# Turning queries and keys of a cross-decoder by VectorE squares and ScalarE copies instead of TensorE transposes

## The chip, the cores and the metric

The kernel runs as one program on one core of a Trainium2 chip. The metric is the device time of that program in microseconds (us). A core has a matrix engine (TensorE, PE in the profile; its weight loads are PEld), a vector engine (VectorE, DVE), a scalar engine (ScalarE, ACT), a general engine (GpSimd, POOL) and a sequencer that here only issues transfers (SyncE, SP). Each engine works through its own list of instructions in order, and semaphores join them.

## The reference, cut to what matters

A decoder trunk of two layers works on 256 tokens of width 2048, in fp32. Layer 0 is gated linear attention with a gated ConvFFN. Layer 1, where the change lies, makes shared keys and values from the output of layer 0 and attends to them, again with a ConvFFN behind. With 256 tokens there is one block of keys, so its attention is plain causal attention of 16 heads of width 128 with a bias by distance:

```python
kv = rms_norm(x, norm_w) @ w_kv;  k, v = split(kv)
k = rms_norm(k.reshape(B, S, 16, 128), k_norm_w)          # norm over each head's 128
q = rms_norm((rms_norm(x, norm_w) @ w_q).reshape(B, S, 16, 128), q_norm_w) * 128 ** -0.5
s = einsum(q, k) + bias_table[:, rel_bucket(t - j)]       # causal: -inf where j > t
o = einsum(softmax(s), v).reshape(B, S, 2048) @ w_out
```

The scores need queries and keys with the head's 128 elements on the partitions, while the projections leave them with tokens on the partitions. So each head's queries and keys are turned (transposed), 256 tokens by 128 each.

## The kernel before

**The stream of weights.** All weights come in halves of 128x1024 by transfers that SP issues into `wraw` (ten buffers). Each half is split for TensorE: ACT makes the high part `whi` (a cast, L143), DVE the rest `wlo` (L145). Both parts have four buffers. One half is one step of `gemm_tok` (L376): eight matmuls of 128x512 with `whi` (L385), then four with `wlo` (L388). ACT's cast for a step can be up to four steps ahead; with four buffers, it waits for the end of the `whi` matmuls of four steps earlier.

**The order of the work around the stream.** `step()` (L354) runs the jobs that have come due and then hands out the split half. `after(n, job)` makes a job due n steps later; `after_high()` and `after_low()` order what is issued inside them behind the newest cast or the newest rest. From the program in this order, a scheduler fixes the list of each engine before the program runs; a job's place in an engine's list can so be several steps from the step that issued it. An engine that waits in its list holds everything behind it.

**Layer 1's projections.** A group is eight steps and makes 512 columns for 256 tokens, in one of three accumulators `acc` of two banks each. Counted from the first step of the queries, groups Q0 to Q3 are steps 0 to 31 (operand `xw`), K0 to K3 steps 32 to 63 and V0 to V3 steps 64 to 95 (both on the operand `xkv`, which is made from `h` late in the queries, L255 and L259), and from step 96 on `project` multiplies the attention's output `ox` by the output weights: step 96+j reads `ox` of head pair j.

**What follows a group.** After a query or key group, `head_norm` takes the columns out of the accumulator (ACT: L1043 squares, L1044 copies, twice each), sums the squares (DVE L1046, L1047), takes the power (POOL L1049, tile `rr`) and multiplies (DVE L1051). Three and four steps after the group's end `features` turns two heads each: four TensorE transposes (L1059) into the bank `tr`, which ACT (L1062, L1064) and DVE (L1065) take out as a whole fp32 part and as a high and a low part. `kqw`, which holds both norms' weights and the scale, is applied to the keys there. `softmax` follows 5 to 8 steps after a key group (four matmuls, L1075 and L1077, on DVE the bias L1084, on ACT the exponentials L1086, on DVE a reciprocal L1088 and two scalings L1090). `turn` transposes the probabilities in 32x32 squares on DVE (L1099) and lets POOL send them to DRAM and back (`turned`, L1102; `pT`, L1103), and `weights` splits them (ACT L436 and L1115, DVE L437).

After a value group, `v_out` takes the columns out of the accumulator (ACT L483, DVE L484, ACT L486, tiles `vm`), and `values` forms 16 matmuls for each pair of head pairs (L490 to L493, bank `o`), whose result is split into `ox` (ACT L436, DVE L437).

**Squares.** A helper `squares` (L410), used before for other tiles, turns four 128x256 heads without TensorE: two DVE transposes of 32x32 squares (L415), then 16 copies of 32x256, which move each square to its place (L398, in four rows of four). With `spread` the copies are ACT's and come due a row a step from two steps later; without it they are POOL's.

Of the kernel before, what the change touches and what calls it, by code (L numbers as in the profile page):

```python
# [8 lines left out]
F32 = mybir.dt.float32  # L9
F32R = mybir.dt.float32r  # L10
I32 = mybir.dt.int32
AF = mybir.ActivationFunctionType
OP = mybir.AluOpType
# [5 lines left out]
S = 256  # L19
# [26 lines left out]
LAG = 8  # L46
# [109 lines left out]
def trunk(ctx: ExitStack, tc: tile.TileContext, xT, cst, msk, w1p, w2a, w_k, w_qa, w_v2, w_v, w_gt, w_g, w_got, w_go,  # L156
          w_up0, w_dn0, w_kk, w_kv, w_mq, w_mot, w_mo, w_up1, w_dn1, rel, onehot, out):
    nc = tc.nc
    V, A, T = nc.vector, nc.scalar, nc.tensor
# [11 lines left out]
    def slot(shape, dt, name):  # L171
        return big.tile(shape, dt, name=name, tag="slot")

    def temp(name, shape=(128, 2, S), dt=F32):
        return tmp.tile(list(shape), dt, name=name, tag="temp")

    def bank(name, shape):
        return mis_ps.tile(list(shape), F32, name=name, tag="bank")
# [6 lines left out]
    for layer, todo in enumerate(ahead):  # L185
        t = dram.tile([len(todo), 128, 2048], F32, name=f"tsum{layer}")
# [20 lines left out]
    kqw = keep.tile([128, 1], F32, name="kqw")  # L207
# [36 lines left out]
    ident = mk[:, 0:128]  # L244
# [73 lines left out]
    def after(steps, job):  # L318
        later.append((cur[0] + steps, job))
# [28 lines left out]
    def after_high():  # L348
        return tc.issue_after(ws.high.ins)

    def after_low():
        return tc.issue_after(ws.low.ins)
# [40 lines left out]
    def square(y, x, spread=False):  # L393

        def row(m, copy):
            xs_ = x[32 * m:32 * m + 32].rearrange("a t (n c b) -> a n t c b", c=4, b=32)
            for c in range(4):
                copy(y[32 * c:32 * c + 32, :, :, 32 * m:32 * m + 32], xs_[:, :, :, c])  # L398

        def row_behind(m):  # L400
            with after_high():
                row(m, A.copy)

        for m in range(4):
            if spread:
                after(2 + m, lambda m=m: row_behind(m))
            else:
                row(m, nc.gpsimd.tensor_copy)

    def squares(name, xs):  # L410

        x, y = slot([128, 2, 512], F32, name + "T"), slot([128, 4, S], F32, name)
        for t in range(2):
            with after_low():
                V.transpose(x[:, t], xs[t])  # L415
        square(y.rearrange("p n (t s) -> p n t s", t=2), x)
        return y

    def rows(xs):
        return lambda kt: xs[kt // 2][:, kt % 2, :]  # L420

    def both(ps, name):
        t = temp(name)
        A.copy(t, ps[:, :, S:])
        V.tensor_add(t, t, ps[:, :, :S])
        return t
# [8 lines left out]
    def split(dst_hi, dst_lo, src):  # L435
        A.copy(dst_hi, src)  # L436
        V.tensor_sub(dst_lo, src, dst_hi.bitcast(F32))  # L437
# [36 lines left out]
    xs = rows(nrm.xs)  # L474
# [81 lines left out]
    for hd in (2, 3):  # L556
        ps = gemm_tok(xs)
# [9 lines left out]
    for hd in range(GH):  # L567
        ps = gemm(xs, KT)
        rstd = nrm.rstd
        k = both(ps, "k")  # L570
# [66 lines left out]
    for hd in range(GH):  # L637
        ps = gemm(xs, KT)
        q = both(ps, "q")
# [32 lines left out]
    for g in (0, 1, 3):  # L672
        ps = gemm_tok(xs)
        after(0, lambda g=g, ps=ps: gate_turn(g, ps))
    for p in (4, 5):
        ps = gemm(xs, KT)
        g = both(ps, "g")
# [361 lines left out]
    def head_norm(ps, name):  # L1039
        t_, sq = slot([128, 2, 512], F32, name), slot([128, 2, 512], F32, "hsq")  # L1040
        for t in range(2):
            r = n_q.col[:, t:t + 1]
            A.activation(sq[:, t, :], ps[:, t, :], AF.Square, scale=r)  # L1043
            A.activation(t_[:, t, :], ps[:, t, :], AF.Copy, scale=r)  # L1044
        ss = small.tile([128, 8], F32, name="ss")
        V.tensor_reduce(ss, sq.rearrange("p t (h d) -> p (t h) d", d=128), axis=AX.X, op=OP.add)  # L1046
        V.tensor_scalar(ss, ss, 1.0 / 128, EPS, op0=OP.mult, op1=OP.add)  # L1047
        rr = small.tile([128, 8], F32, name="rr")
        nc.gpsimd.tensor_tensor(rr, ss, mhalf, op=OP.pow)  # L1049
        u = t_.rearrange("p t (h d) -> p (t h) d", d=128)  # L1050
        V.tensor_mul(u, u, rr[:, :, None].to_broadcast([128, 8, 128]))  # L1051
        return t_

    def features(t_, c, f, scale, c0):

        tp = bank("tr", (128, 2, S))
        for i in range(2):
            for t in range(2):
                T.transpose(tp[:, i, 128 * t:128 * t + 128],  # L1059
                            t_[:, t, (2 * c + i) * 128:(2 * c + i + 1) * 128], ident)  # L1060
        whole, halves_ = f[0][:, 2 * c:2 * c + 2, :], f[1][c]
        A.activation(whole, tp[:, :, :128], AF.Copy, scale=scale)  # L1062
        hi, lo = halves_[:, :, 0, :], halves_[:, :, 1, :]
        A.activation(hi, tp[:, :, c0:], AF.Copy, scale=scale)  # L1064
        V.scalar_tensor_tensor(lo, tp[:, :, c0:], scale, hi.bitcast(F32), op0=OP.mult, op1=OP.subtract)  # L1065

    qf, kf, ox = [], [], []
    pts = [None] * MH
# [2 lines left out]
    def softmax(hd):  # L1071
        (q0, q1), (k0, k1) = qf[hd // 4], kf[hd // 4]
        q1, k1 = q1[hd // 2 % 2][:, hd % 2], k1[hd // 2 % 2][:, hd % 2]
        sp = bank("s", (128, 384))
        T.matmul(sp[:, 0:128], q0[:, hd % 4, :], k0[:, hd % 4, :], start=True, stop=True)  # L1075
        for i, (a, b) in enumerate(((0, 0), (0, 1), (1, 0))):
            T.matmul(sp[:, 128:384], q1[:, a, :], k1[:, b, :], start=i == 0, stop=i == 2)  # L1077
        s = temp("s", (128, 384))
        st = small.tile([128, 4], F32, name="st")
        bt = bias[hd // 4][:, hd % 4, :]  # L1080
        for t, (c0, c1) in enumerate(((0, 128), (128, 384))):
            n = c1 - c0
            rev = bass.AP(tensor=bt.tensor, offset=bt.offset + n - 1, ap=[bt.ap[0], [-1, n]])
            V.tensor_tensor_reduce(s[:, c0:c1], sp[:, c0:c1], rev, -1.0, 3.0e38, OP.add, OP.min,  # L1084
                                   st[:, t:t + 1])
            A.activation(s[:, c0:c1], s[:, c0:c1], AF.Exp, bias=st[:, t:t + 1], scale=-1.0,  # L1086
                         accum_out=st[:, 2 + t:3 + t])
        V.reciprocal(st[:, 2:4], st[:, 2:4])  # L1088
        for t, (c0, c1) in enumerate(((0, 128), (128, 384))):
            V.tensor_scalar(s[:, c0:c1], s[:, c0:c1], st[:, 2 + t:3 + t], None, op0=OP.mult)  # L1090
        pts[hd] = s
# [3 lines left out]
    def turn(hd):  # L1095

        t = slot([128, 2, 384], F32, "pT")
        with tc.issue_after(ws.low.ins):
            V.transpose(t[:, 0], pts[hd])  # L1099
        to = turned[hd].rearrange("f b (m a) -> m b f a", a=32)  # L1100
        for m in range(4):
            nc.gpsimd.dma_start(to[m], t[32 * m:32 * m + 32, 0].rearrange("b (f a) -> b f a", a=32))  # L1102
        nc.gpsimd.dma_start(t[:, 1].rearrange("k (j q) -> k j q", j=3),  # L1103
                            turned[hd].rearrange("(j f) b q -> (f b) j q", f=4))
        pts[hd] = t[:, 1]

    def weights(hd):
        tp = pts[hd]
        if hd % 8 == 0:
            p1s.append(slot([128, 8, 128], F32, "p1"))  # L1110
        if hd % 2 == 0:
            p0s.append(slot([128, 2, 2, S], F32R, "p0"))
        with tc.issue_after(ws.high.ins):
            split(p0s[-1][:, hd % 2, 0], p0s[-1][:, hd % 2, 1], tp[:, :256])
            A.copy(p1s[-1][:, hd % 8], tp[:, 256:])  # L1115
# [16 lines left out]
    xs = rows(n_q.xs)  # L1132
    for g in range(4):
        ps = gemm_tok(xs)
        t_ = head_norm(ps, "q")
        if g % 2 == 0:
            q8 = slot([128, 8, 128], F32, "q0")
        q1 = slot([128, 4, 2, 128], F32R, "q1")
        f = (q8[:, g % 2 * 4:g % 2 * 4 + 4], (q1[:, 0:2], q1[:, 2:4]))
        qf.append(f)  # L1140
        for c in range(2):
            after(3 + c, lambda t_=t_, c=c, f=f: features(t_, c, f, 1.0, 128))
    xs = rows(xkv)
    for g in range(4):
        ps = gemm_tok(xs)
        t_ = head_norm(ps, "k")
        if g % 2 == 0:
            k8 = slot([128, 8, 128], F32, "k0")
        f = (k8[:, g % 2 * 4:g % 2 * 4 + 4], [slot([128, 2, 2, S], F32R, f"k1{c}") for c in range(2)])
        kf.append(f)  # L1150
        for c in range(2):
            after(3 + c, lambda t_=t_, c=c, f=f: features(t_, c, f, kqw, 0))
        for i in range(4):
            after(5 + i, lambda i=i, g=g: softmax(4 * g + i))
            after(7 + i, lambda i=i, g=g: turn(4 * g + i))
            after(15 + i, lambda i=i, g=g: weights(4 * g + i))
    for g in range(4):
        ps = gemm_tok(xs)
        if g % 2 == 0:
# [126 lines left out]
```

## Time and profile before

| | |
|---|---|
| Median of 3 runs | 2169.63 us (2169.37 to 2171.07) |
| The profiled execution | 2170.52 us, its span 2168.8 us, granted TensorE clock 1.0 |
| TensorE busy | 2160.1 us, 100% of the span |
| VectorE busy | 1749.0 us, 81% |
| ScalarE busy | 1535.0 us, 71% |
| GpSimd busy | 351.5 us, 16% |
| TensorE on the chain that ended last | 99% |

Busy time says how much an engine worked over the whole span. The chain is followed back from the last instruction, at each step to what released it, and says which work set the end. The profiled execution ended 0.9 us above the median of the runs; a sum made from its rows is compared with its own time.

### The profile page before, as it was taken

Reading aid. Unit: us, or ns where it says so; the run is one execution under the profiler, and the core shown is the slowest. Engines: PE = TensorE matmul, PEld = TensorE weight load, DVE = VectorE, ACT = ScalarE, POOL = GpSimd, SP = SyncE. Lnnn points to the kernel's source line nnn. Section 1 sums busy time; section 2 is a strip of 40 time slices with the busy share of each in tenths; the row PEclk is TensorE's granted clock in tenths of the full one; section 3 lists DMA queues with packets and bytes.
Section 4 is the critical chain, followed back from the end, with each engine's and each line's share of the span. In section 5 each row is a group of like instructions: output and inputs, shape, how many; then the busy total and the mean of one; then the engine's idle time right before and its main releaser. Section 6 shows DMA issues by size and latency. Waiting matters only on the chain.

```text
span 2168.8 us, 30105 instructions
## 1 busy us (share of the span) xinstructions
PE 2160.1 (100%) x9936; PEld 1801.4 (83%) x9936; DVE 1749.0 (81%) x2525; ACT 1535.0 (71%) x2448; POOL 351.5 (16%) x519
## 2 busy tenths in 40 slices
PE   9999999999999999999999999999999999999999
PEld 7888888888888888888888888888888888888887
DVE  7676788778788887988977787587887888779898
ACT  6655554698899886767656575456888898967575
POOL 0000347100000004300002343150000000043000
PEclk9999999999999999999999999999999999999999
DMA  9586678978888886897968898779888888869996
GB/s 333 192 280 211 233 270 268 338 261 274 295 279 302 289 274 205 317 338 273 403 215 283 278 311 288 249 236 317 276 292 299 283 299 293 269 202 337 335 355 259
DMA packets 193600, 613.11 MB, mean 283 GB/s; under 512 B 38257, under 2 KB 38785, under 8 KB 193442
## 3 DMA queue, kind: packets, MB, share of 16 engines
q1 hardware_dynamic: 166322, 523.78, 71.1%
q0 software_dynamic: 26400, 86.60, 10.7%
q8 instruction: 78, 1.28, 0.2%
q10 hardware_dynamic: 720, 0.79, 0.1%
q14 instruction: 80, 0.66, 0.1%
HBM read 535.31 MB, written 75.78 MB: 282 GB/s over the span
## 4 chain that ended last, share of the span: by engine, by line
PE 99%; DMA 0%; DVE 0%; POOL 0%; issue 0%; SPq 0%; ACT 0%; POOLq 0%
PE acc L385 46%; PE acc L388 23%; PE acc L857 15%; PE p L857 6%; PE acc L370 5%; PE acc L372 2%; DMA wraw<-w_v 0%; PE sT L607 0%; PE tr L1059 0%; PE s L1077 0%; PE z L513 0%; PE o L493 0%; PE s L1075 0%; PE oT L493 0%; DVE wlo L145 0%; PE oT L492 0%
## 5 line engine op out<-in xcount | busy, mean ns | idle before, releaser
L145 DVE TENSOR_TENSOR wlo<-wraw,whi 128x1024 fp32r<-128x1024 f32 (+1 forms) x788 | 927.3, 1188 | 316.9 <-ACT whi L143 267.0
L143 ACT CAST whi<-wraw 128x1024 fp32r<-128x1024 f32 (+1 forms) x788 | 792.1, 1015 | 445.8 <-PE acc L385 262.5
L385 PE MATMUL acc<-whi,xw 128*128 128x512 f32 x3520 | 873.9, 390 | 1.4 <-ACT whi L143 1.2
L385 PEld LDWEIGHTS acc<-whi,xw 128*128 128x128 f32 x3520 | 659.7, 188 | 138.5 <-ACT whi L143 1.6
L388 PE MATMUL acc<-wlo,xw 128*128 128x512 f32 x1760 | 472.3, 389 | 0.0
L388 PEld LDWEIGHTS acc<-wlo,xw 128*128 128x128 f32 x1760 | 330.2, 188 | 68.4
L398 ACT COPY up<-uT 32x256 f32<-32x256 f32 x608 | 245.4, 404 | 8.5 <-DVE uT L776 1.0
L339 POOL DMA_DIRECT2D tsum<-ahead x116 | 62.6, 540 | 967.0 <-DVE ahead L327 563.5
L857 PE MATMUL acc<-whi,hid 128*128 128x512 f32 x588 | 167.6, 390 | 0.0
L145 DVE TENSOR_TENSOR wlo<-ahead,whi 128x1024 fp32r<-128x1024 f32 x98 | 120.5, 1232 | 17.4 <-ACT whi L143 11.1
L143 ACT CAST whi<-ahead 128x1024 fp32r<-128x1024 f32 x98 | 102.5, 1053 | 41.3 <-PE acc L857 19.8
L385 PE MATMUL acc<-whi,xkv 128*128 128x512 f32 x512 | 129.7, 391 | 0.0
L857 PEld LDWEIGHTS acc<-whi,hid 128*128 128x128 f32 x588 | 110.1, 188 | 22.6
L857 PE MATMUL p<-whi,hid 128*128 128x512 f32 x356 | 112.1, 389 | 0.0
L385 PEld LDWEIGHTS acc<-whi,xkv 128*128 128x128 f32 x512 | 95.3, 188 | 18.9
L857 PE MATMUL acc<-whi,comb 128*128 128x512 f32 x348 | 101.3, 389 | 0.0
L857 PE MATMUL acc<-wlo,hid 128*128 128x512 f32 x294 | 96.2, 389 | 0.0
L789 ACT ACTIVATE au<-up,cs 128x256 f32<-128x256 f32 x176 | 95.7, 593 | 0.0
L398 POOL COPY up<-uT 32x256 f32<-32x256 f32 x96 | 72.2, 752 | 96.4 <-DVE uT L776 74.1
L796 DVE SCALAR_TENSOR_TENSOR au<-up,cs,au 128x254 f32<-128x254 f32 x176 | 80.7, 483 | 0.0
L326 DVE TENSOR_TENSOR ahead<-ahead 128x512 f32<-128x512 f32 x116 | 80.2, 691 | 0.0
L327 DVE TENSOR_TENSOR ahead<-ahead 128x512 f32<-128x512 f32 x116 | 79.7, 687 | 0.1
(283 smaller groups left out, 2409.2 us busy)
## 6 DMA issues: line engine op xcount, KB each, us to landing
wraw<-w_up SPq DMA_DIRECT2D x352, 512.0 KB, 5.9
wraw<-w_dn SPq DMA_DIRECT2D x118, 512.0 KB, 6.4
ahead<-w_dn SPq DMA_DIRECT2D x116, 512.0 KB, 6.1
tsum<-ahead POOLq DMA_DIRECT2D x116, 512.0 KB, 6.1
ahead<-tsum SPq DMA_DIRECT2D x98, 512.0 KB, 6.1
wraw<-w_mq SPq DMA_DIRECT2D x32, 512.0 KB, 5.9
wraw<-w_kk SPq DMA_DIRECT2D x32, 512.0 KB, 6.3
wraw<-w_kv SPq DMA_DIRECT2D x32, 512.0 KB, 5.7
```

Source lines behind the costliest of these rows:

```text
L143: self.high = nc.scalar.copy(hi[:, a:b], src[:, a:b])
L145: self.low = nc.vector.tensor_sub(lo[:, a:b], src[:, a:b], hi[:, a:b].bitcast(F32))
L326: jobs = [lambda: V.tensor_sub(b22, b22, b12), lambda: V.tensor_sub(b12, b12, b11), lambda: V.tensor_add(b11, b22, b11), lambda: V.tensor_ ...
L327: lambda: V.tensor_add(b11, b22, b11), lambda: V.tensor_sub(b21, b21, b11)]
L339: nc.gpsimd.dma_start(parked[layer][at][:, o:o + 1024], t)
L370: T.matmul(ps[:, b, :], two[i][0][:, c:c + 128], xs(kt), start=kt == 0, stop=False)
L385: T.matmul(ps[:, t, :], xs(kt)[:, x0 + 128 * t:x0 + 128 * t + 128], hi[:, c:c + 512], start=kt == 0 and x0 == 0, stop=False)
L388: T.matmul(ps[:, t, :], xs(kt)[:, 128 * t:128 * t + 128], lo[:, c:c + 512], start=False, stop=kt == KT - 1)
L398: copy(y[32 * c:32 * c + 32, :, :, 32 * m:32 * m + 32], xs_[:, :, :, c])
L789: A.activation(au[:, i, :], t[:, i, :], AF.Identity, bias=col(cb + n), scale=col(cw + 2 * 2 * FT + n))
L796: V.scalar_tensor_tensor(au[:, i, 2:], t[:, i, :S - 2], col(cw + n), au[:, i, 2:], op0=OP.mult, op1=OP.add)
L857: T.matmul(p[n], x[xi], w[wi][:, 512 * f:512 * f + 512], start=n not in begun, stop=left[n] == 0)
```

## The change

`head_norm` ends with `squares` for the turned tile: two DVE transposes and 16 ACT copies per group, with `spread`. `features` with its TensorE transposes is gone. In its place `query_part` (ACT L1059 and L1060, DVE L1062) and `key_part` (ACT L1069, DVE L1071) make the parts from the turned tile, eight and nine steps after the group (`LAG` is 8). The turned keys are used as the whole part directly, and `kqw` is applied to the queries. `softmax`, `turn` and `weights` come due 10, 12 and 20 steps after a key group, in place of 5, 7 and 15.

```diff
-        square(y.rearrange("p n (t s) -> p n t s", t=2), x)
+        square(y.rearrange("p n (t s) -> p n t s", t=2), x, spread)
...
         V.tensor_mul(u, u, rr[:, :, None].to_broadcast([128, 8, 128]))
-        return t_
-    def features(t_, c, f, scale, c0):
-        tp = bank("tr", (128, 2, S))
-        for i in range(2):
-            for t in range(2):
-                T.transpose(tp[:, i, 128 * t:128 * t + 128],
-                            t_[:, t, (2 * c + i) * 128:(2 * c + i + 1) * 128], ident)
-        whole, halves_ = f[0][:, 2 * c:2 * c + 2, :], f[1][c]
-        A.activation(whole, tp[:, :, :128], AF.Copy, scale=scale)
+        return squares(name, [t_[:, t] for t in range(2)], True)
+
+    def query_part(y, c, whole, halves_):
+        heads_ = y[:, 2 * c:2 * c + 2]
         hi, lo = halves_[:, :, 0, :], halves_[:, :, 1, :]
-        A.activation(hi, tp[:, :, c0:], AF.Copy, scale=scale)
-        V.scalar_tensor_tensor(lo, tp[:, :, c0:], scale, hi.bitcast(F32), op0=OP.mult, op1=OP.subtract)
+        with after_high():
+            A.activation(whole[:, 2 * c:2 * c + 2, :], heads_[:, :, :128], AF.Copy, scale=kqw)
+            A.activation(hi, heads_[:, :, 128:], AF.Copy, scale=kqw)
+        with after_low():
+            V.scalar_tensor_tensor(lo, heads_[:, :, 128:], kqw, hi.bitcast(F32), op0=OP.mult, op1=OP.subtract)
+    def key_part(y, c, halves_):
...
+        with after_high():
+            A.copy(hi, heads_)
+        with after_low():
+            V.tensor_sub(lo, heads_, hi.bitcast(F32))
...
-            after(3 + c, lambda t_=t_, c=c, f=f: features(t_, c, f, 1.0, 128))
+            after(LAG + c, lambda y=y, c=c, f=f: query_part(y, c, f[0], f[1][c]))
...
-            after(5 + i, lambda i=i, g=g: softmax(4 * g + i))
-            after(7 + i, lambda i=i, g=g: turn(4 * g + i))
-            after(15 + i, lambda i=i, g=g: weights(4 * g + i))
+            after(LAG + 2 + i, lambda i=i, g=g: softmax(4 * g + i))
+            after(LAG + 4 + i, lambda i=i, g=g: turn(4 * g + i))
+            after(LAG + 12 + i, lambda i=i, g=g: weights(4 * g + i))
```

The lists of the engines change in many places between step 11 and the first steps of `project`; behind that they are as before. Three places follow. In the rows, an operation is followed by its output, `<-` and its inputs; x8 means eight in a row, and a number on a name tells one buffer's contents from another's.

TensorE, before, from the first query group's transposes (`tr`) on:

```order
L385 MATMUL acc<-whi,xw 128x512 x8
L1059 MATMUL tr<-mk,q 128x128 x4
L388 MATMUL acc<-wlo,xw 128x512 x4
L385 MATMUL acc<-whi,xw 128x512 x8
L388 MATMUL acc<-wlo,xw 128x512 x4
```

TensorE at the same place now:

```order
L385 MATMUL acc<-whi,xw 128x512 x8
L388 MATMUL acc<-wlo,xw 128x512 x4
L385 MATMUL acc<-whi,xw 128x512 x8
L388 MATMUL acc<-wlo,xw 128x512 x4
L385 MATMUL acc<-whi,xw 128x512 x3
```

The transposes are gone from TensorE's list here and at the eight other places where they stood.

ScalarE at the end of the queries, before: the casts of the stream, the takeout of the turned third query group (`tr`) and the operand `xkv` for the keys.

```order
L255 ACTIVATE xkv<-h,cs 128x256 x4
L143 CAST whi<-wraw 128x1024 x4
L1062 ACTIVATE q_10741<-tr 128x256
L1064 ACTIVATE q_10742<-tr 128x2x128
L255 ACTIVATE xkv<-h,cs 128x256 x6
L1062 ACTIVATE q_10741<-tr 128x256
L1064 ACTIVATE q_10742<-tr 128x2x128
L255 ACTIVATE xkv<-h,cs 128x256 x2
L143 CAST whi<-wraw 128x1024 x4
```

ScalarE there now; the two casts ahead of the copies end with that for step 32, the first of the keys, and the three behind begin with that for step 33.

```order
L143 CAST whi<-wraw 128x1024 x2
L398 COPY q<-qT 32x8x32 x4
L255 ACTIVATE xkv<-h,cs 128x256 x2
L398 COPY q<-qT 32x8x32 x4
L255 ACTIVATE xkv<-h,cs 128x256 x2
L398 COPY q<-qT 32x8x32 x4
L255 ACTIVATE xkv<-h,cs 128x256 x2
L398 COPY q<-qT 32x8x32 x4
L255 ACTIVATE xkv<-h,cs 128x256 x4
L143 CAST whi<-wraw 128x1024 x3
```

Between two casts now stand 16 copies and ten activations, where there were twelve activations.

ScalarE in the value groups, before, where V0's accumulator is taken out (`vm_12210`, `vm_12209`), some ten steps after V0 ended:

```order
L143 CAST whi<-wraw 128x1024
L1115 COPY p_12159<-pT 128x128
L1086 ACTIVATE s,st<-s,st 128x256
L483 ACTIVATE vm_12210<-acc,col_h 128x512
L143 CAST whi<-wraw 128x1024
L1115 COPY p_12159<-pT 128x128
L486 ACTIVATE vm_12209<-acc,col_h 128x512
```

ScalarE there now (`vm_12220`, `vm_12219`); the first cast is that for step 91, which waits for the `whi` matmuls of step 87.

```order
L143 CAST whi<-wraw 128x1024
L1092 ACTIVATE s,st<-s,st 128x128
L1092 ACTIVATE s,st<-s,st 128x256
L483 ACTIVATE vm_12220<-acc,col_h 128x512
L486 ACTIVATE vm_12219<-acc,col_h 128x512
L1069 CAST k_12225<-k 128x2x256
```

TensorE there now: the first matmuls of V0 (`o`) stand right behind the last four of step 87, ahead of V3, whose accumulator is V0's.

```order
L388 MATMUL acc<-wlo,xkv 128x512 x4
L490 MATMUL o<-p_11772,vm_12220 128x256
L491 MATMUL o<-p_11772,vm_12220 128x256
L1081 MATMUL s<-k,q_10759 128x128
L492 MATMUL o<-p_11772,vm_12220 128x256
L493 MATMUL o<-p_11771,vm_12219 128x128
```

The same four for the pair's second head follow, and then step 88. The takeout of V0 has moved to just ahead of V3 on ScalarE, and TensorE's first use of it stands at the start of V3. In the same way V2's matmuls (`vm_12706`) stand right ahead of step 100, the fifth of `project`, which reads their result.

More of the change, by code (lines that the diff above doesn't have):

```diff
@@ L408, in square, with squares @@
                 row(m, nc.gpsimd.tensor_copy)
-    def squares(name, xs):
+    def squares(name, xs, spread=False):
         x, y = slot([128, 2, 512], F32, name + "T"), slot([128, 4, S], F32, name)
@@ L1051, in head_norm @@
         V.tensor_mul(u, u, rr[:, :, None].to_broadcast([128, 8, 128]))
-        return t_
-    def features(t_, c, f, scale, c0):
-        tp = bank("tr", (128, 2, S))
-        for i in range(2):
-            for t in range(2):
-                T.transpose(tp[:, i, 128 * t:128 * t + 128],
-                            t_[:, t, (2 * c + i) * 128:(2 * c + i + 1) * 128], ident)
-        whole, halves_ = f[0][:, 2 * c:2 * c + 2, :], f[1][c]
-        A.activation(whole, tp[:, :, :128], AF.Copy, scale=scale)
-        hi, lo = halves_[:, :, 0, :], halves_[:, :, 1, :]
-        A.activation(hi, tp[:, :, c0:], AF.Copy, scale=scale)
-        V.scalar_tensor_tensor(lo, tp[:, :, c0:], scale, hi.bitcast(F32), op0=OP.mult, op1=OP.subtract)
+        return squares(name, [t_[:, t] for t in range(2)], True)
+    def query_part(y, c, whole, halves_):
+        heads_ = y[:, 2 * c:2 * c + 2]
+        hi, lo = halves_[:, :, 0, :], halves_[:, :, 1, :]
+        with after_high():
[4 more added lines that the diff above has]
+    def key_part(y, c, halves_):
+        heads_ = y[:, 2 * c:2 * c + 2]
+        hi, lo = halves_[:, :, 0, :], halves_[:, :, 1, :]
+        with after_high():
+            A.copy(hi, heads_)
+        with after_low():
+            V.tensor_sub(lo, heads_, hi.bitcast(F32))
     qf, kf, ox = [], [], []
@@ L1074, in softmax @@
         sp = bank("s", (128, 384))
-        T.matmul(sp[:, 0:128], q0[:, hd % 4, :], k0[:, hd % 4, :], start=True, stop=True)
+        T.matmul(sp[:, 0:128], q0[:, hd % 4, :], k0[:, hd % 4, :128], start=True, stop=True)
         for i, (a, b) in enumerate(((0, 0), (0, 1), (1, 0))):
@@ L1134, in trunk @@
         ps = gemm_tok(xs)
-        t_ = head_norm(ps, "q")
+        y = head_norm(ps, "q")
         if g % 2 == 0:
@@ L1145, in trunk, with part @@
         ps = gemm_tok(xs)
[L1146 to L1150, printed above, removed]
+        y = head_norm(ps, "k")
+        k1 = []
+        kf.append((y, k1))
         for c in range(2):
-            after(3 + c, lambda t_=t_, c=c, f=f: features(t_, c, f, kqw, 0))
+            def part(y=y, c=c, k1=k1):
+                k1.append(slot([128, 2, 2, S], F32R, f"k1{c}"))
+                key_part(y, c, k1[c])
+            after(LAG + c, part)
         for i in range(4):
-            after(5 + i, lambda i=i, g=g: softmax(4 * g + i))
-            after(7 + i, lambda i=i, g=g: turn(4 * g + i))
-            after(15 + i, lambda i=i, g=g: weights(4 * g + i))
+            after(LAG + 2 + i, lambda i=i, g=g: softmax(4 * g + i))
+            after(LAG + 4 + i, lambda i=i, g=g: turn(4 * g + i))
+            after(LAG + 12 + i, lambda i=i, g=g: weights(4 * g + i))
     for g in range(4):
```

## The prediction

> **What bounds the kernel now.** I read the page first: its busy times, then the shares of the chain that ended last, then the costliest groups.
>
> ```profile
> PE 2160.1 (100%) x9936; PEld 1801.4 (83%) x9936; DVE 1749.0 (81%) x2525; ACT 1535.0 (71%) x2448; POOL 351.5 (16%) x519
> ...
> PE 99%; DMA 0%; DVE 0%; POOL 0%; issue 0%; SPq 0%; ACT 0%; POOLq 0%
> ...
> L145 DVE TENSOR_TENSOR wlo<-wraw,whi 128x1024 fp32r<-128x1024 f32 (+1 forms) x788 | 927.3, 1188 | 316.9 <-ACT whi L143 267.0
> L143 ACT CAST whi<-wraw 128x1024 fp32r<-128x1024 f32 (+1 forms) x788 | 792.1, 1015 | 445.8 <-PE acc L385 262.5
> ```
>
> TensorE is the bound: it is busy all the time, so what leaves its list shortens the run, and a wait that makes it idle lengthens it. The other two matter where they make TensorE wait. ScalarE's idle time ahead of the casts mostly ends with a TensorE matmul: it waits for a free buffer, which means that the splitting runs ahead by as much as four buffers allow. VectorE's idle time ahead of its rests ends with ScalarE's cast. So the question about each added ScalarE stretch is whether that lead covers it.
>
> **What leaves TensorE.** The chain of the stage of queries and keys shows the transposes (L1059), 64 in nine pieces; here are the two pieces of four, two of the seven pieces of eight, and two plain pieces, which make up one step.
>
> ```profile
> 1126.81 0.44 PE tr L1059 x4
> 1137.99 0.59 PE tr L1059 x4
> 1171.19 0.87 PE tr L1059 x8
> 1206.97 1.81 PE acc L385 x8
> 1208.78 0.91 PE acc L388 x4
> 1309.21 0.88 PE tr L1059 x8
> ```
>
> A step is 1.81 + 0.91 = 2.72 us. The pieces of four cost 0.44 and 0.59 us; six pieces of eight cost 0.87 each (5.2 us), and the seventh stands at 1155 us, behind a wait. In that place the chain leaves TensorE, and the timeline gives the idle time:
>
> ```profile
> 1152.34 1.67 POOL rr L1049
> 1154.04 1.24 DVE q L1051
> 1155.32 1.09 PE tr L1059 x8
> ```
>
> ```profile
> 1151.58 0.75 POOL L1035 DMA_DIRECT2D bias<-bscr  x1 [5.17 <-PE acc L388]
> 1155.32 1.09 PE L1059 MATMUL tr<-mk,q 128*128 128x128 f32 x8 [1.09 <-DVE q L1051]
> ```
>
> GpSimd was held by the transfer of the bias, so the power came late, then the multiplication, and TensorE idled 1.09 us before its transposes, which themselves took 1.09. Now nobody on TensorE waits for that multiplication so soon: its readers are VectorE's squares, and the query parts are due eight steps, 22 us, after their group. So the wait goes and nothing is late next on TensorE there. The gain: 0.44 + 0.59 + 5.2 + 1.09 + 1.09 = **8.4 us**.
>
> The row for the scores' matmuls stays; that they run some five steps later costs TensorE nothing by itself, since it has the same matmuls to run.
>
> **What ScalarE gets.** Per group 16 copies, in all 128; it loses 32 activations that took `tr` out, and gets 16 for the queries and 8 casts for the keys in their place. The prices, first from the up-projection's own copies, then from the stage of the queries, are:
>
> ```profile
> 1536.55 3.32 ACT L398 COPY up<-uT 32x256 f32<-32x256 f32 x8
> ...
> 1161.32 1.71 ACT L255 ACTIVATE xkv<-h,cs 128x256 fp32r<-128x256 f32 x4
> ...
> 1197.94 1.05 ACT L143 CAST whi<-wraw 128x1024 fp32r<-128x1024 f32 x1 [1.48 <-PE acc L385]
> 1200.66 1.05 ACT L143 CAST whi<-wraw 128x1024 fp32r<-128x1024 f32 x1 [1.67 <-PE acc L385]
> ```
>
> Eight copies take 3.32 us, 0.415 each, so a group's 16 take **6.6 us**. The casts come every 2.72 us, and 1.67 of that is idle: ScalarE waits for step s-4's `whi` matmuls. From the end of the `whi` matmuls that release the cast of step s-1 to the start of step s, TensorE has 0.91 + 4 x 2.72 = 11.8 us of work; less these two casts of 1.05 us, other work of up to **9.7 us** between them is covered. In the lists the 16 copies of a group mostly stand in one run between two casts, with up to 1.7 us of other work: seven of eight groups are covered, by 1.4 to 3.1 us. These copies cost nothing as long as that lead is there; without it their excess falls on TensorE one for one.
>
> The exception is the third query group's, between the casts of steps 32 and 33: 16 copies and ten `xkv` activations. Four of the latter took 1.71 us, so ten take some 4.2: in all 10.8 us, 1.1 above the cover. The first copy also waits for VectorE's two transposes, whose price is:
>
> ```profile
> L415 DVE STREAM_TRANSPOSE outT<-acc x12: 672/690/717, 324.6 to 1448.2; 128x512 f32<-128x512 f32 x12
> ```
>
> Two of them stand behind a rest of 1.2 us there; I reckon the wait for them from nothing to 2.2 us, and take 1.2. So TensorE waits 1.1 to 3.3 us ahead of step 33; I take **2.3 us**.
>
> [...]
>
> VectorE gets two transposes per group (1.4 us) and keeps 16 low parts. In the fullest window of the stage it is busy 20.70 of 22 us:
>
> ```profile
> 1281.00:1303.00 22.00, 22.00 (x109) 18.56 (x108) 20.70 (x50) 15.21 (x37) 13.26 (x19) 1.00 0.92 315
> ```
>
> That would fill it, but the softmaxes now stretch over more steps (50 to 93 in the list, before 46 to 80), which takes about a third of their work out of such a window. I cost it at nothing; what hides it is the same lead of four buffers.
>
> **What is moved.** The softmaxes, the squares of the probabilities and their transfers run five or more steps later, into the value groups. With them ScalarE's takeouts of V0 and V2 move behind later casts, as the order shows. Before, V0's began about 28 us ahead of the step 88 that needs its accumulator. ScalarE's timeline there, which also prices a head's two exponentials (from 1317.39 to 1318.29, 0.90 us):
>
> ```profile
> 1317.39 0.40 ACT L1086 ACTIVATE s<-s,st 128x128 f32<-128x128 f32 x1 [1.50 <-DVE st L1084]
> ...
> 1318.29 0.39 ACT L1086 ACTIVATE s<-s,st 128x128 f32<-128x128 f32 x1
> ...
> 1320.31 0.67 ACT L483 ACTIVATE vm<-acc,col_h 128x512 fp32r<-128x512 f32 x1
> ...
> 1322.49 0.68 ACT L486 ACTIVATE vm<-acc,col_h 128x512 f32<-128x512 f32 x1
> ```
>
> The other prices: VectorE's scalings and transposes of the probabilities, its share of the takeout, and TensorE's first two matmuls of V0, 0.11 apart.
>
> ```profile
> L1090 DVE TENSOR_SCALAR s<-s,st x32: 244/346/507, 1224.4 to 1328.4; 128x128 f32<-128x128 f32 x16, 128x256 f32<-128x256 f32 x16
> L1099 DVE STREAM_TRANSPOSE pT<-s x16: 529/572/581, 1225.0 to 1330.9; 128x384 f32<-128x384 f32 x16
> ```
>
> ```profile
> L484 DVE SCALAR_TENSOR_TENSOR vm<-acc,col_h,vm x4: 743/748/751, 1321.0 to 1378.1; 128x512 fp32r<-128x512 f32 x4
> ```
>
> ```profile
> 1329.53 0.28 PE L490 MATMUL o<-p,vm 128*128 128x256 f32 x1
> 1329.64 0.28 PE L491 MATMUL o<-p,vm 128*128 128x256 f32 x1
> ```
>
> Step 88, from the end of step 87's `whi` matmuls, which frees the cast of step 91. ScalarE: cast 1.05, exponentials 0.90, L483 0.67, done at 2.6. VectorE: after the cast the rest (1.19, done at 2.2), then in its list four scalings (1.4) and two transposes of probabilities (1.1), done at 4.8, then L484 (0.75), done at 5.5. Then ScalarE's L486 (0.68), done at 6.2. TensorE had 0.91 of `wlo` and five matmuls of 0.12, so from about 1.5 on it waits, in one piece or two: 4.7 us. Neighbours on ScalarE and VectorE start 0.1 us before the one ahead ends (the exponentials above do), so I take **4.4 us**. Behind L486 on ScalarE stand two casts of keys and the takeout of `ox`, then the cast of step 92, which has three steps of lead left.
>
> Step 100, from the end of step 99's `whi` matmuls, goes the same way. ScalarE: cast 1.05, two copies of probabilities (at most 0.40 each, by the exponential of that size), L483, done at 2.5. VectorE: the rest done at 2.2, an addition of 128x512 (0.75, taken as L484's), a split of 128x256 (at most 0.5, by the scalings' row) and L484, done at 4.2; then ScalarE's L486, done at 4.9; TensorE is ready at 1.6. That is 3.3 less the same overlaps: **2.8 us**. At step 96 the sum comes out at 0.1 us, at step 102 at none.
>
> The sum: 2.3 + 4.4 + 2.8 + 0.1 = 9.6 lost against 8.4 won, **1.2 us** longer. Against the profiled execution's 2170.5 that is 2171.7; that one stood 0.9 above the median, so I forecast **2171 us**. A measurement of this kernel can tell about 0.2% from no change, 4.3 us: so "the same" is 2165.3 to 2174.0.
>
> **The rivals.**
> - *Faster: the two waits among the value groups do not come.* If VectorE has done its softmax part before TensorE reaches steps 88 and 100, or other waits push the takeouts ahead, the loss is 2.3 to 2.5: 2169.6 - 6.0 = 2163.6. It decides only when those two together cost under 1.7 us. For it speaks that takeouts before lay 28 us ahead; against it, that the order has the wait in every list it passes, and an engine cannot overtake in its own list. Chance 0.16.
> - *Slower: the copies are not covered.* ScalarE becomes the bound in the key groups, when VectorE hands over the turned squares late. Margins of 1.4 to 3.1 us are left beside seven runs of copies; the squares (1.4), the multiplication (1.24) and a rest (1.19) ahead of them are 3.8 us, so a run that waits for all three overruns by 0.8 to 2.4. Three such runs cost some 4.5 us, 2175.5. It decides from 3 us in all. For it speaks the VectorE window at 20.70 of 22; against it, that the copies come due two steps after their squares. Chance 0.17. [...]
> - *Slower: the probabilities come back late.* ScalarE splits the last heads' probabilities just ahead of V2's takeout, so they must have landed. The transfers' medians are:
>
> ```profile
> turned<-pT POOLq DMA_DIRECT2D x64, 48.0 KB, 4.9
> pT<-turned POOLq DMA_DIRECT2D x16, 192.0 KB, 6.3
> ```
>
> In series 11.2 us; by the lists the last head's squares are done about 14 us ahead of that split, 3 us of margin. GpSimd issues three heads' transfers in a row there; if one more return, 6.3, comes between, TensorE waits 3.3 longer at step 100, 2174.3. It decides from a lateness of 6 us. Chance 0.12.
>
> **How the numbers follow.** The forecast has 0.55, and its own bounds are those of its terms: 1.1 to 3.3, 2 to 5, 1 to 4 for the three waits, so 2167 to 2175. The first rival's 0.16 is faster, the other two's 0.29 slower; part of the forecast's upper end is counted with them. The range reaches from the first rival's time to beyond the second's, 2163.5 to 2177, and leaves out all waits gone (2161) and both slow rivals together.
>
> **What would show it.** Right: no `tr` in the trace, no idle TensorE near 1155; in the waits, TensorE idle ahead of step 33 behind ScalarE's cast by 2.3 us, ahead of step 88's first matmuls behind VectorE's L484 or ScalarE's L486 by some 4 us, and of step 100's by some 3. TensorE's busy time falls by about 7 us and its idle time grows by about as much. Wrong: copies on ScalarE faster or slower than 0.415 us apart, TensorE idle behind casts at other groups, or a chain through `pT` at step 100. If the span shortens by 6 us or more, the two waits in the value groups are not there, and the reading of the order is at fault.

## The result, and the profile after

The changed kernel took 2190.93 us in the median of 4 runs (2188.69 to 2192.94), the kernel before 2169.74 (4 runs): a ratio of 1.0097 with a 95% interval of 1.0085 to 1.0109. It is 21 us slower, and lies outside the range. The profiled execution ended at 2192.94 us, the slowest of the four, with a span of 2191.1 us against 2168.8.

The page of the changed kernel, the line of busy times and that of the granted TensorE clock in 40 slices:

```profile
PE 2164.9 (99%) x9872; PEld 1800.3 (82%) x9872; DVE 1754.4 (80%) x2541; ACT 1583.1 (72%) x2568; POOL 355.8 (16%) x519
...
PEclk9999999999999999999999999999999999999999
```

The 64 transposes are gone (9872 matmuls, before 9936), yet TensorE is busy 4.8 us longer, although 7.3 us of work left it. Its idle time, span less busy time, went from 8.7 to 26.2 us. So the 22.3 us of the span are: 7.3 less for the transposes, some 12.1 more for the other matmuls, 17.5 more idle. The page's slices show no fall of the clock, since they are 55 us wide. The windows of 22 us do (the column behind POOL's):

```profile
1149.00:1171.00 22.00, 19.43 (x77) 15.01 (x76) 12.90 (x16) 14.92 (x28) 5.21 (x5) 0.92 0.79 275
...
1347.00:1369.00 22.00, 15.71 (x66) 12.69 (x65) 15.33 (x40) 10.79 (x24) 12.29 (x19) 0.77 0.86 277
```

In these and in two more (0.92 and 0.84) the granted clock is low, where every window of the stage before had 1.00, and these four hold all of TensorE's waits but two, of 1.54 and 0.15 us. The waits of TensorE from the queries to the project stage, summed by what ended them:

```profile
PE o L490 <- ACT vm L483: 5.6, 2, 3.0
PE acc L385 <- ACT whi L143: 4.6, 2, 2.7
PE o L492 <- DVE vm L484: 3.3, 2, 3.2
PE o L493 <- ACT vm L486: 1.6, 2, 1.4
PE s L1081 <- DVE st L1090: 1.5, 1, 1.5
PE acc L388 <- DVE wlo L145: 0.7, 1, 0.7
```

That is 17.3 us. The same view of the kernel before has 1.1 us, the one wait for the multiplication. Three of the places are those of the prediction (steps 33, 88 and 100, the fourth, step 96, is 0.15); the first is not. It is near step 25. GpSimd's, VectorE's, ScalarE's and TensorE's timelines there:

```profile
1150.26 0.75 POOL L1035 DMA_DIRECT2D bias<-bscr  x1 [5.59 <-PE acc L385]
1151.02 1.66 POOL L1049 TENSOR_TENSOR rr<-ss,mhalf 128x8 f32<-128x8 f32 x1
```

```profile
1152.72 1.23 DVE L1051 TENSOR_TENSOR q<-q,rr 128x1024 f32<-128x1024 f32 x1 [8.11 <-POOL rr L1049]
...
1155.60 1.30 DVE L415 STREAM_TRANSPOSE qT<-q 128x512 f32<-128x512 f32 x2
```

```profile
1149.86 1.06 ACT L143 CAST whi<-wraw 128x1024 fp32r<-128x1024 f32 x1 [1.66 <-PE acc L385]
1156.93 6.63 ACT L398 COPY q<-qT 32x256 f32<-32x256 f32 x16 [6.02 <-DVE qT L415]
```

```profile
1158.85 1.21 PE L388 MATMUL acc<-wlo,xw 128*128 128x512 f32 x4 [0.70 <-DVE wlo L145]
...
1164.68 3.50 PE L385 MATMUL acc<-whi,xw 128*128 128x512 f32 x8 [1.87 <-ACT whi L143]
1167.98 1.31 PE L388 MATMUL acc<-wlo,xw 128*128 128x512 f32 x4
```

The late power is still there. Before, TensorE itself waited 1.09 us for what follows from it. Now VectorE waits 8.11 us for it with its rests queued behind, and the 0.70 us of TensorE are for one of these. ScalarE waits 6.02 us for the squares, then copies for 6.63 (16 at 0.414, as forecast), and 12.7 us lie between two casts, 3 above the cover of 9.7; the 1.87 us of TensorE are for the cast behind. Then see TensorE's last rows: eight matmuls take 3.30 us from start to start (1164.68 to 1167.98), where 1.81 is usual.

At step 88, ScalarE and VectorE read:

```profile
1351.87 0.67 ACT L483 ACTIVATE vm<-acc,col_h 128x512 fp32r<-128x512 f32 x1
1356.83 0.69 ACT L486 ACTIVATE vm<-acc,col_h 128x512 f32<-128x512 f32 x1 [4.29 <-DVE vm L484]
```

```profile
1351.14 1.22 DVE L145 TENSOR_TENSOR wlo<-wraw,whi 128x1024 fp32r<-128x1024 f32 x1
1352.28 0.76 DVE L437 TENSOR_TENSOR p<-pT,p 128x256 fp32r<-128x256 f32 x2
...
1354.22 0.99 DVE L1096 TENSOR_SCALAR s<-s,st 128x128 f32<-128x128 f32 x4
1355.13 1.04 DVE L1105 STREAM_TRANSPOSE pT<-s 128x384 f32<-128x384 f32 x2
1356.08 0.72 DVE L484 SCALAR_TENSOR_TENSOR vm<-acc,col_h,vm 128x512 fp32r<-128x512 f32 x1
```

The chain is the one foreseen, with VectorE later than reckoned: it still had the rest of the step before (1351.14) and a split of probabilities when the cast of step 91 was done. TensorE waited 2.98 + 3.16 = 6.1 us for 4.4 foreseen. At step 100, ScalarE waited three times for returned probabilities (the first and the last of them here), two of them right ahead of a part of V2's takeout, which was the third rival's mechanism:

```profile
1399.03 0.41 ACT L436 CAST p<-pT 128x256 fp32r<-128x256 f32 x1 [1.59 <-DMA pT<-turned]
...
1404.20 0.40 ACT L436 CAST p<-pT 128x256 fp32r<-128x256 f32 x1 [1.67 <-DMA pT<-turned]
```

### The profile page after: what moved, and what is told of

The parts are those of the page before. It is cut to its first block, busy times and chain, and to the rows that moved or that the text cites. A ratio compares the mean times of both kernels' runs of the same rounds, so it can differ in the third digit from the quotient of the medians.

```text
span 2191.1 us, 30098 instructions
## 1 busy us (share of the span) xinstructions
PE 2164.9 (99%) x9872; PEld 1800.3 (82%) x9872; DVE 1754.4 (80%) x2541; ACT 1583.1 (72%) x2568; POOL 355.8 (16%) x519
```

## The experiments

Two questions came out of this: why the takeouts and the copies are late, and why the matmuls behind the waits are slow. The theory for the first is the **full pool**: queries, keys, their scratch, the turned tiles, probabilities and takeouts all come out of one pool of 32 tiles of 4 KB a partition, and a group of the change takes two more (a key group has half a tile back, since its whole part needs none of its own) and holds them longer. A tile that has to wait for another's release is late, and what follows it in the lists is late too. Its rivals are the lags by themselves and the copies by themselves.

**Tiles reused.** The squares write into the tile of the squared columns, the copies back into the normalised tile.

```diff
-        return squares(name, [t_[:, t] for t in range(2)], True)
+        y = t_.rearrange("p t d -> p (t d)").rearrange("p (n s) -> p n s", s=S)
+        for t in range(2):
+            with after_low():
+                V.transpose(sq[:, t], t_[:, t])
+        square(y.rearrange("p n (t s) -> p n t s", t=2), sq, True)
+        return y
```

> The change with one difference: the two VectorE squares write into the tile of the squared columns, which nobody reads any more, and the 16 copies write back into the normalised tile, so a group takes two tiles from the pool of 32 and not four. Theory of the full pool: V0's and V2's takeouts came late because their tiles had to wait for one that the turned keys held; with tiles free they stand eight to ten steps earlier, the waits ahead of steps 88 and 100 (10.6 us idle and some 7 us of slow matmuls behind them) go, and so does the one ahead of step 33, since the copies and the operand xkv no longer stand in one stretch: 2165 to 2168 us, with the wait near step 25 still there. Rival, the later softmaxes: the lags by themselves push the takeouts behind ScalarE's other work, pool or not: 2187 us or more.

Measured: 2168.69 us, ratio to before 0.9993 (0.9983 to 1.0002), so 22 us better than the change with the same instructions on every engine. The waits of TensorE from the queries to the project stage:

```profile
PE s L1086 <- ACT k L398: 1.3, 2, 0.9
PE acc L385 <- ACT whi L143: 1.2, 2, 0.6
PE acc L388 <- DVE wlo L145: 1.1, 1, 1.1
PE s L1086 <- DVE st L1095: 0.2, 1, 0.2
```

All waits for takeouts are gone, and the granted clock is 1.00. Of the wait near step 25, 1.1 us are left, at step 28; small waits for the copies of the keys and the casts behind them came beside, and the time ended 0.7 above the forecast.

**Bias by SyncE.**

```diff
-            nc.gpsimd.dma_start(t, bass.AP(tensor=s.tensor, offset=s.offset + 4 * g * 384,
+            nc.sync.dma_start(t, bass.AP(tensor=s.tensor, offset=s.offset + 4 * g * 384,
```

> The change with the four transfers of the bias table issued by SyncE and not by GpSimd. Theory of the held power: GpSimd waits for these transfers and so gives the power of Q1 late, the squares and the 16 copies behind it are late, and the cast behind the copies makes TensorE wait twice near step 25 (2.6 us idle, then some 1.7 us of slow matmuls): about 2186.6 us, and no idle TensorE there. Rival, the 16 copies are too long a stretch by themselves: the wait stays, 2190 to 2191 us.

Measured: 2187.44 us (2183.12 to 2188.41), against 2190.93 for the change. In its trace TensorE has no wait before step 33. So some 3.5 us of the loss were the held power (4.8 us between the two profiled executions). That 16 copies in a row are too long by themselves is refuted here; with their squares on time they are covered.

**Both.** The two edits together.

> Both edits together. If both theories hold, what is left is the gain alone: 8.4 us under the kernel before, 2161 to 2162 us, with TensorE idle nowhere in the queries, keys and values. If the copies are an uncovered load in themselves, 2168 us or more.

Measured: 2166.05 us (10 runs) against 2170.07 (25 runs), ratio 0.9981 (0.9972 to 0.9991): the best of the versions tried, 4.0 us under the kernel before, and 4.4 us short of the 8.4 expected. Its waits:

```profile
PE o L490 <- ACT vm L483: 1.3, 1, 1.3
PE acc L385 <- ACT whi L143: 0.9, 2, 0.6
PE s L1086 <- ACT k L398: 0.9, 1, 0.9
PE s L1086 <- DVE st L1095: 0.2, 1, 0.2
```

These 3.3 us are most of what is missing in the profiled execution, which took 2167.38 us. TensorE's busy time fell by 5.8 (2160.1 to 2154.3) and not by 7.3; of the other 1.5, 0.5 lies in the matmuls of the scores (9.68 us from start to start, 9.21 before), and where the rest lies stayed open. The first line is still a wait for a takeout, V2's, at step 94: right ahead of it ScalarE waited 5.41 and 1.76 us for returned probabilities, so this one is the third rival's mechanism.

**The lags alone**, in the kernel before:

```diff
-            after(5 + i, lambda i=i, g=g: softmax(4 * g + i))
-            after(7 + i, lambda i=i, g=g: turn(4 * g + i))
-            after(15 + i, lambda i=i, g=g: weights(4 * g + i))
+            after(10 + i, lambda i=i, g=g: softmax(4 * g + i))
+            after(12 + i, lambda i=i, g=g: turn(4 * g + i))
+            after(20 + i, lambda i=i, g=g: weights(4 * g + i))
```

> The kernel before, with its TensorE transposes, but with the softmaxes, turns and weights five steps later, as in the change. Theory of the full pool: the lags alone take few tiles more, the takeouts of the values stand where they stood, so the same as before, 2168 to 2172 us. Rival, the lags: the waits ahead of steps 88 and 100 come as in the change, some 17 us, about 2187 us.

Measured: 2169.67 us, ratio 1.0003 (0.9993 to 1.0012). The lags cost nothing by themselves.

**Only the scratch tile saved**: as the first experiment, but `y = slot([128, 4, S], F32, name)`.

> The change with only the scratch tile saved: the VectorE squares write into the tile of the squared columns, and the turned tile stays one of its own. Theory of the full pool: one tile less for each group is enough for the takeouts of V0 and V2, which the lists now place at the casts of steps 79 to 81 and 96 and 97, so no idle time ahead of steps 88 and 100. The list still has 10.0 us of copies and xkv ahead of the cast of step 32, and GpSimd still holds the power of Q1, so those two waits stay: 2168 to 2173 us. Rival, that it was the copies and not the pool: 2185 us or more.

Measured: 2174.27 us (2172.52 to 2175.36), 1.3 above the range given, and 16.7 below the change. No wait for a takeout is left; the copies' waits are:

```profile
PE acc L385 <- ACT whi L143: 5.2, 4, 3.2
PE s L1086 <- ACT k L398: 1.7, 1, 1.7
```

One tile a group decides on the value groups; the second one on the copies.

**Six tiles withheld**, in the kernel before:

```diff
+    kept = [slot([128, 2, 512], F32, "kept") for _ in range(6)]
+    for k_ in kept:
+        V.memset(k_[:, 0, 0:1], 0.0)
     xs = rows(n_q.xs)
...
+    seen = small.tile([128, 1], F32, name="seen", bufs=1)
+    with after_low():
+        for k_ in kept:
+            V.tensor_copy(seen, k_[:, 0, 0:1])
     n_ffn = Norm(C_FN + KT, "xw", rows=False)
```

> The kernel before, with its TensorE transposes and its lags, but six of the 32 tiles of the pool taken at the start of the queries and given back behind the values (a few VectorE writes and reads of one column beside). Theory of the full pool: the list places V0's takeout behind the cast of step 91, as in the change, and TensorE waits ahead of step 88 by 4 to 7 us, with 1.5 to 3 us of slow matmuls behind it: 2175 to 2182 us. Rival, the takeouts come late only through the changed work: the same as before, 2168 to 2172 us.

Measured: 2175.41 us, ratio 1.0026 (1.0015 to 1.0037). The kernel before, with nothing of the change in it, gets the change's wait at step 88, for the same takeout, though smaller (1.83 us here, and 0.85 in two more pieces behind it, 2.7 in all for the 4 to 7 expected):

```profile
1348.81 0.39 PE L490 MATMUL o<-p,vm 128*128 128x256 f32 x1 [1.83 <-ACT vm L483]
```

There is no wait at step 100. With this the full pool is shown from both sides for V0's takeout: it begins at 1320.31 us in the kernel before, at 1351.87 with the change, at 1316.24 with the tiles reused, at 1321.14 with the lags alone and at 1348.08 with six tiles withheld. For V2's takeout only the one side is shown: with tiles given back, 1.3 us or nothing is left of its wait.

**One step later**, on the version with both edits (softmax, turn and weights at `LAG` + 3, 5 and 13).

> Both edits (tiles reused, bias by SyncE) with the softmaxes, turns and weights one step later still, since there TensorE waited 0.9 us for ScalarE's copies of the keys and then 0.4 and 0.6 us for casts. If these small waits are all that is left of the change, up to 2 us less than with both edits alone: 2164 to 2166 us; if they only move, the same 2166.

Measured: 2168.67 us, 2.6 above the version with both edits (each against its own runs of the kernel before: 0.8 under it, and 4.0 under it). The wait for ScalarE's copies grew from 0.9 to 1.9 us. So these small waits are not due to lags that are too short; what sets them stayed open.

**Pauses of TensorE.** For the second question, TensorE was made to wait in the second up-projection of the kernel before, where nothing else of the change is near: ahead of the fifth step of eight groups.

```diff
+    def pause(xs):
+        at = newest[0].ins
+        with tc.issue_after(at):
+            g0 = bank("g0", (128, 128))
+            T.matmul(g0, ones, held, start=True, stop=True)
+        V.tensor_copy(held, g0)
+        for _ in range(14):
+            V.tensor_copy(held, held)
+        with tc.issue_after(at):
+            g1 = bank("g1", (128, 512))
+            for _ in range(36):
+                T.matmul(g1, ones, xs(0), start=True, stop=True)
+            end = T.matmul(g1[:, :128], ones, held, start=True, stop=True)
+        return tc.issue_after(end.ins)
```

The short pauses have neither of the two loops, the long ones the first, the filled ones both (with 14, then 36 matmuls).

> The kernel before with eight short pauses of TensorE in the second up-projection, 16 steps apart: a small matmul, one VectorE copy of its result, a small matmul that reads the copy, and only then the next step. Each pause costs its own length, 1 to 3 us by what VectorE has ahead of it. Theory of the clock: below some 1.5 us of idle time the next matmuls run at the usual 0.227 us each, so the time grows by the idle time and no more. Rival, no effect of the clock: the same.

> The same eight pauses made longer by 14 further VectorE copies in a row, so that TensorE idles 3 to 6 us each time. Theory of the clock: behind each pause the granted clock is low for 2 to 5 us, and the time grows by the idle time plus 1.5 to 3 us for each pause, 12 to 24 us in all. Rival: the time grows by the idle time alone.

> The long pauses with 14 matmuls of 128x512 that nobody reads inside each of them, 3.2 us of TensorE work each. Theory of the clock: TensorE stays at full clock, so although it does more work the kernel is faster than the one with the bare long pauses, by most of the 12 to 24 us. Rival: the same time as with the bare pauses, or longer.

> The long pauses, which measured 8 to 10 us of idle time each, now filled with 36 matmuls of 128x512 (8.2 us of TensorE work) instead of 14, which had left 5 to 6 us idle. Theory of the clock: no idle time above 1.5 us is left, the matmuls behind the pauses run at the usual pace, and the time is 1.5 to 2.5 us for each pause below that of the bare long pauses, 2240 to 2250 us. Rival, the idle time has nothing to do with the slow matmuls behind it: 2257 us or more.

Measured: short 2190.23 us, long 2260.27, filled with 14 2258.27, filled with 36 2244.32 (before 2169.45). TensorE's timeline behind a short pause of 1.45 and one of 2.71 us, behind a long one, and behind one filled with 36 matmuls:

```profile
1704.23 0.33 PE L392 MATMUL g<-held,ones 128*128 128x128 f32 x1 [1.45 <-DVE held L385]
1704.40 2.04 PE L405 MATMUL acc<-whi,xw 128*128 128x512 f32 x8
...
1799.17 0.47 PE L392 MATMUL g<-held,ones 128*128 128x128 f32 x1 [2.71 <-DVE held L385]
1799.44 3.72 PE L405 MATMUL acc<-whi,xw 128*128 128x512 f32 x8
1802.96 1.91 PE L408 MATMUL acc<-wlo,xw 128*128 128x512 f32 x4
```

```profile
1682.81 0.45 PE L392 MATMUL g<-held,ones 128*128 128x128 f32 x1 [9.50 <-DVE held L387]
1683.06 3.73 PE L405 MATMUL acc<-whi,xw 128*128 128x512 f32 x8
1686.58 1.91 PE L408 MATMUL acc<-wlo,xw 128*128 128x512 f32 x4
```

```profile
1679.55 0.33 PE L392 MATMUL g<-held,ones 128*128 128x128 f32 x1 [0.95 <-DVE held L387]
1679.71 2.07 PE L405 MATMUL acc<-whi,xw 128*128 128x512 f32 x8
```

Behind 1.45 us the eight take 2.04 us up to the end of the last, behind 2.71 and 9.50 us 3.72 and 3.73; from start to start the latter are 3.52 us, 0.44 a matmul (0.43 behind the first) where 0.23 is usual. The long pauses were longer than meant, 8.3 to 9.6 us, so 14 matmuls still left 4.9 to 6.2 us idle, and that kernel won next to nothing on the clock (the matmuls behind a pause lost 1.8 us, against 2.0); its expectation failed on the size of the pause. With 36, at most 1.05 us stayed idle, the matmuls behind ran at full pace, and the kernel is 16.0 us faster than the one with bare pauses, although TensorE does 65 us more work. Of these 2.0 us a pause, 0.16 is a pause that came out shorter (9.26 against 9.42 from its first small matmul to the next step); about 1.8 is the clock.

## Why the prediction was wrong

**The gain was right in kind, and not shown in full.** 64 transposes and the 1.09 us wait of TensorE are gone. The version with both edits has kept 4.0 us of the 8.4, and its busy time fell by 5.8 where the transposes were priced at 7.3.

**"The wait goes and nothing is late next" failed.** The prediction looked for the next reader of the late multiplication on TensorE and found none; it did not add the late power to the 6.6 us of copies in ScalarE's list, although it named the held power and reckoned with the cover of 9.7. 6.02 + 6.63 is above it, and TensorE waited 1.87 us for the cast behind, after 0.70 for a rest that VectorE had queued behind the same multiplication. Taking the bias off GpSimd's queue gave 3.5 us back.

**The price of a wait failed most.** Each wait was put at its idle time. Behind every wait of 1.87 us or more the matmuls ran at half pace for a while, and that is 10.5 of the 12.1 us of extra busy time: with the tiles reused, the same instructions at full clock keep TensorE busy for 2154.4 us and not 2164.9. It is three fifths of what the added idle time itself came to. In the stage, the trace of before has only one wait, of 1.09 us, and its matmuls behind it at full pace, so it says nothing of longer waits; the prediction ought to have left the upper end open for waits longer than any that the trace showed.

**The three terms were mis-sized, all to the low side.** Step 33: 2.70 for 2.3, inside its bounds. Step 88: 6.1 for 4.4, above its bound of 5, since VectorE was a rest behind. Step 100: 2.65 + 0.18 + 1.44 = 4.3 for 2.8, above its bound of 4, since the probabilities came late as in the third rival. Step 96: 0.15 for 0.1. One of 1.5 us at step 59, for a bank of scores that VectorE freed late, was not in the sum: VectorE's load was put at nothing, because the softmaxes' longer stretch would take a third of their work out of a window; by the prediction's own steps, 34 stretched to 43, it is a fifth. Together, with the 2.6 us near step 25, 17.3 idle for 9.6.

**Reading the order held, and gave the wrong cause.** Every place named had its wait. But the takeouts were put down to the later softmaxes, and the lags by themselves cost nothing (1.0003); it was the pool. The rivals: that the waits do not come was wrong; that the copies are not covered was right at one place, in a query group and through the late power, and not in the key groups; the late probabilities came, but step 100 grew by 1.5 us for them and not by 3.3.

## What to carry to other kernels

Count the tiles that a change adds to a shared pool, and how long each lives, before its instructions: here one scratch tile a group, reused instead of new, was worth 16.7 of the 21 us lost. When a wait leaves one engine's list, look which list it is in now, and add it to whatever else that list holds between two casts. Where TensorE is the bound, price a wait at its length and at what the matmuls behind it lose: in these traces nothing behind a wait of 1.54 us or less that stood alone, and 1.4 to 2.9 us behind one of 1.87 us or more. Waits that stand close count together: 1.74 and 0.86 us, 0.7 apart, had slow matmuls behind them too, in the version with the scratch tile saved.

## What the runs showed of the hardware

In the changed kernel the granted clock fell from 1.00 to 0.50 behind the waits of 1.87, 2.70, 2.98 and 2.65 us. Over the traces, pauses of 0.38 and 1.45 us (the short pauses), 0.95 and 1.05 (filled with 36 matmuls), 1.32 (both edits) and 1.54 (the change) that stood alone left the pace as it was; those of 1.87 and 2.70 (the change), 2.71 (the short pauses) and more halved it, for 1.4 to 2.9 us of lost time, 2.9 behind one of 9.50 us as behind one of 2.71. The length of a single wait did not tell by itself: one of 1.86 us, in the version one step later, left the pace, and in the version with the scratch tile saved 1.74 and 0.86 us, 0.7 apart, halved it.

What told these cases apart is how the idle time lay to the instants at which the clock changed. In the changed kernel it fell at 1165.04, 1188.93, 1352.77 and 1403.97 us of the trace, which lie 7, 48 and 15 times 3.413 us apart, and it stayed low for 3.41, 3.41, 10.24 and 6.83 us. Cut at these instants and in steps of 3.413 us from them, stretches of the trace read as follows (behind the comma TensorE's busy time, third from the end the granted clock). The wait of 1.87 us and the clock behind it, then the wait of 1.54:

```profile
1161.62:1165.04 3.42, 1.55 (x8) 0.97 (x7) 0.38 (x1) 3.35 (x7) 0.00 (x0) 1.00 1.00 370
1165.04:1168.45 3.41, 3.41 (x10) 2.64 (x9) 2.68 (x3) 3.41 (x7) 0.00 (x0) 0.50 0.90 315
1168.45:1171.86 3.41, 3.41 (x16) 2.80 (x15) 2.89 (x4) 3.41 (x6) 1.66 (x1) 1.00 0.74 261
...
1264.02:1267.43 3.41, 1.87 (x9) 1.08 (x7) 3.41 (x11) 1.98 (x6) 1.41 (x3) 1.00 0.36 123
```

The kernel before with six tiles withheld, at its waits of 1.83, 0.50 and 0.35 us:

```profile
1348.05:1351.46 3.41, 1.80 (x9) 1.22 (x9) 3.41 (x14) 3.41 (x13) 2.69 (x5) 1.00 0.96 337
1351.46:1354.88 3.42, 3.42 (x17) 3.23 (x16) 2.69 (x8) 1.40 (x3) 1.33 (x3) 0.50 0.30 92
```

The version one step later, cut in the same steps counted back from the fall of the clock at the end of the program (in the changed kernel that fall, at 2189.03 us, lies 230 steps behind the one at 1403.97). Here a stretch ends inside the wait of 1.86 us, and 1.2 us of idle time fall on either side (behind it with the wait of 0.58 that follows):

```profile
1245.06:1248.48 3.42, 2.20 (x10) 1.50 (x8) 1.56 (x7) 3.33 (x11) 1.79 (x3) 1.00 0.07 14
1248.48:1251.89 3.41, 2.19 (x9) 1.73 (x10) 3.14 (x10) 3.36 (x10) 2.10 (x5) 1.00 0.27 57
```

In the changed kernel, cut so from 30 us behind its start to 8 us ahead of its end, the stretches at full clock with 1.87, 2.21, 2.70 and 2.98 us idle had the fall at their ends; no other had more than 1.54 us idle, and none of these had one. With six tiles withheld 1.61 of 3.41 us were idle ahead of the fall. In the kernel before, where TensorE waited once in the stage, for 1.09 us, the clock was 1.00 up to 2167.50 us of its 2168.8. At half clock the matmuls of 128x512 behind the pauses started 0.44 us apart, at full clock 0.23.

ScalarE's 16 copies of 32x256 behind the late squares took 6.63 us in the changed kernel, 0.414 each, as the row of before had it (eight in 3.32 us).
